# Block 1's small matrix products issued as wholes, one microsecond behind the weight products

## The chip, the cores and the metric

The kernel is one program on one core of a Trainium2 chip. Its engines work side by side: PE multiplies matrices, ACT and DVE work on elements, POOL does a few scalars, SP issues the transfers from memory. The metric is the time of one execution in microseconds (us) on the device, lower is better. The kernel before takes 1691.05 us (median of 3 runs, 1690.16 to 1691.24).

## What is computed

Two layers of a "first block" and two of a "second block" on 256 tokens of width 1024, in float32. The change concerns the first half of the first block, the mixer, which occurs twice (once a layer):

```
h = rmsnorm(x, g_pre_mix);  z = h @ w_in            # 1024 -> 2660 columns
o_moba = softmax attention(rope(qa), rope(ka), va)  # 4 heads of 64, causal
log_f  = log_sigmoid(z_fg + b_forget);  cum = cumsum(log_f, tokens)
o_fox  = softmax attention(qb, kb, vb, + cum[t] - cum[s])
o_mla  = softmax attention from low-rank q and k,v (rmsnorm, w_mla_q_up, w_mla_kv_up)
o_dil  = dilated attention, one masked softmax      # 4 heads of 64
x = x + rmsnorm(concat(o_moba, o_fox, o_mla, o_dil) @ w_out, g_post_mix)
```

Behind it comes a gated feed-forward layer, and the two layers of the second block follow with feed-forward, convolution and pooling. With 256 tokens in tiles of 128, each of the four attentions has two halves of queries, h = 0 (128 keys) and h = 1 (256 keys): eight attentions in a mixer.

## The kernel before, in words

Weights are float32. Each weight unit (128 x 1024) is fetched by SP into a `raw` tile, ACT rounds it to a high part (`wh`), DVE forms the remainder (`wl`), and PE makes three products for one: high by high, high by low, low by high. These are the weight products. Everything else on PE in the mixer is small: transposes against an identity (`idt`, L296), scores q·k (`qk` tiles), weights of the softmax by values (`w` by `vmf`, `vc`, `vd`), and the running sum of the forget gates (`lf` by `cs`).

The order of all instructions is made when the program is built, by a small planner (class `Order`). Every piece of work is a generator that yields one `Op` at a time; the planner keeps a heap, and takes the operation whose start plus `bias` is least, where the start is reckoned from costs written in the code (`mm`, `tr`, `act`, `tt` and so on). Weight products carry a bias of 0.02 (`B_MAIN`); the small products of the mixer carry 0. What comes out is a fixed queue for each engine; on the chip each engine goes through its queue in order, and semaphores hold it where an input is not there yet.

`block1` holds the mixer. Its main generator yields the weight products of each projection (`proj`: latent parts, moba q and k, values of moba and fox, fox q and k, the two low-rank products, dilated q and k, dilated values), then `w_out`, which takes the attentions' outputs in the order moba, fox (h = 0, then 1), low-rank, dilated (h = 0, then 1), 12 weight products each. Chains spawned beside it do the rest: `qkchain`, `foxchain`, `upchain` turn a projection into transposed q and k (`qk`), `cumchain` makes the running sum that fox needs, and `attend` spawns one or two `group`s for each half: scores into a PSUM bank, mask, row maximum, exponentials, reciprocal and scaling into an `lg` tile, transposes into a bank, a copy out of it (`pt`), and then, in `attend`, the products with the values and the split of the result into `mH`, `mL`, which `w_out` reads. There are 8 PSUM banks (`banks`), handed out in the order of asking; the scores of moba and dilated heads use 64 rows of PE each, of alternating halves (`hd % 2`), and the value products 64 columns.

A row of the trace named `lf,cs` is the running sum, `w,vmf` the value products of moba and fox, `w,vc` those of the low-rank attention, `w,vd` of the dilated one. `mH00` is the high part of moba's or fox's output of h = 0.

Of the kernel before, what the change touches and what calls it, by code (L numbers as in the profile page):

```python
# [18 lines left out]
P = 128  # L19
D = 1024  # L20
S = 256
# [11 lines left out]
CST_CAU, CST_DIL, CST_U, CST_IC = 0, 128, 384, 640  # L33
# [10 lines left out]
B_R2 = 0.1  # L44
B_MAIN = 0.02
B_EDGE = -0.1
B_SPLIT = (-0.5, 0.0, 0.2, 0.8)


# [227 lines left out]
def body(ctx, tc, x, positions, wu, wm, wq_up, wkv_up, rows, feat, gfeat, cst, cid, out, nsub=99):  # L277
# [8 lines left out]
    def view(t):  # L286
        return t if isinstance(t, bass.AP) else t[:]

    def mm(o, l, r, start, stop, bias=B_MAIN, fp32=False, half=None):
        o, l, r = view(o), view(l), view(r)  # L290
        c = (4 if fp32 else 1) * r.free_size() / 2400 + 0.0027
        return Op("e", c, (o,), (l, r), lambda: nc.tensor.matmul(o, l, r, start=start, stop=stop), bias, half)  # L292

    def tr(o, i):
        o, i = view(o), view(i)
        return Op("e", 0.1094, (o,), (i,), lambda: nc.tensor.transpose(o, i, idt[:, :P]))  # L296

    def act(o, i, f, bias_=0.0, **kw):
        o, i = view(o), view(i)
        c = (0.052 if i.tensor.name.startswith("bank") else 0.093) + i.free_size() / 1200  # L300
        ins, outs = [i], [o]
        for k in ("scale", "bias"):
            if k in kw and not isinstance(kw[k], float):
                c += 0.093
                ins.append(view(kw[k]))
        if "accum_out" in kw:
            c += 0.093
            outs.append(view(kw["accum_out"]))
        return Op("a", c, outs, ins, lambda: nc.scalar.activation(o, i, f, **kw), bias_, None, f)  # L309
# [72 lines left out]
    cs = one.tile([P, CST_N], F32, name="cs")  # L382
# [12 lines left out]
    def small(n=1):  # L395
        smn[0] += 1
        return smt[smn[0] % len(smt)][:, :n]
# [63 lines left out]
    def split_bias(i):  # L461
        def f():
            ahead = i - st["use"]
            return B_SPLIT[0] if ahead <= 0 else B_SPLIT[1] if ahead < 2 else B_SPLIT[3] if ck.urgent else B_SPLIT[2]
        return f
# [69 lines left out]
    def hidden(n, h, i, src, g):  # L535
# [14 lines left out]
        for j in range(4):  # L550
            kt, o = 4 * i + j, kb[j % 2][:, j * P:(j + 1) * P]
            yield act(hH[:, kt, :], o, AF.Copy, scale=g[:, kt:kt + 1])
            ck.spawn(low(kt, o), bias=B_EDGE)

    def pre_norm(h, n):
# [16 lines left out]

        ts_ = [ck.spawn(part(n, h, i, xx[:, hs[i]], g), bias=B_EDGE) for i in range(2)]
        for t in ts_:
# [10 lines left out]
    def boundary(h, y, half, nxt, eps=None):  # L585
# [8 lines left out]
        a = yield from sumsq(y[0], c / 32)  # L594
        ty = [ck.spawn(gained(0), bias=B_EDGE)]
        a = [a, (yield from sumsq(y[1], c / 32))]
        ms = small()
        yield stt(ms, a[0], c * c * EPS if eps is None else eps, a[1], OP.add, OP.add)
        ty.append(ck.spawn(gained(1), bias=B_EDGE))
        r = small()  # L600
# [3 lines left out]
        if nxt is not None:  # L604
            t = ck.spawn(pre_norm(h, nxt), bias=B_EDGE)
        for i in range(2):
# [53 lines left out]
    def ffn(n_, half, nxt, fp):  # L660
# [117 lines left out]
        for f, c, h in order:  # L778
            yield from f(c, h)
            if f is down and c == NCH - 1:  # L780
                hready[h] = ck.spawn(boundary(h, yacc[h], half, nxt, ep[n_ % 2][h]), bias=B_EDGE)

# [38 lines left out]
    def block1(n_, l, ap, tabs, trope, nxt):  # L821
# [13 lines left out]
        def group(grp, h, q, k, scale, mask, PT, deps, tiled):  # L835
            for t in deps:
                yield t
            nb, hb = h + 1, len(grp)
            wN, w = P * nb, P * nb * hb
            sp = yield banks  # L840
            for i, hd in enumerate(grp):
                yield mm(sp[:, i * wN:(i + 1) * wN], q(hd, h), k(hd, wN), True, True, 0.0, True,
                         hd % 2 if tiled else None)
            lg = yield lgs
            l3 = lg[:, :w].rearrange("p (i n) -> p i n", i=hb)
            s3 = sp[:, :w].rearrange("p (i n) -> p i n", i=hb)
            m = mask[h]
            mN = m.shape[-1]
            mb = m.rearrange("p (o n) -> p o n", o=1).to_broadcast([P, hb, mN])
            if mN < wN:  # L850
                yield act(l3[:, :, :wN - mN], s3[:, :, :wN - mN], AF.Copy)
            yield add(l3[:, :, wN - mN:], s3[:, :, wN - mN:], mb)
            banks.put(sp)
            mx = small(4)
            yield rmax(mx[:, :hb], l3)
            nm = small(4)
            yield ts(nm[:, :hb], mx[:, :hb], -scale, None, OP.mult)
            sm_ = small(4)
            for i in range(hb):
                yield act(l3[:, i, :], l3[:, i, :], AF.Exp, bias=nm[:, i:i + 1], scale=scale,  # L860
                          accum_out=sm_[:, i:i + 1])
            rc = small(4)
            yield recip(rc[:, :hb], sm_[:, :hb])
            for i in range(hb):
                yield ts(l3[:, i, :], l3[:, i, :], rc[:, i:i + 1], None, OP.mult)
            tb = yield banks
            for c in range(hb * nb):
                yield tr(tb[:, c * P:(c + 1) * P], lg[:, c * P:(c + 1) * P])
            lgs.put(lg)
            pt = yield pts  # L870
            yield act(pt[:, :w], tb[:, :w], AF.Copy)
            banks.put(tb)
            for i, hd in enumerate(grp):
                PT[hd] = (pt, i * wN)

        def attend(kt0, h, q, k, v, scale, mask, rowtiled, deps, vdeps, fin):
            if rowtiled:
                groups = [[0, 2], [1, 3]]
            else:
                groups = [[0, 1, 2, 3]] if h == 0 else [[0, 1], [2, 3]]  # L880
            PT = {}
            gs = [ck.spawn(group(g, h, q, k, scale, mask, PT, deps, rowtiled)) for g in groups]
            for t in gs + vdeps:
                yield t
            ob = yield banks
            for s in range(1):
                for hd in range(4):
                    rr = (hd % 2) * 64
                    o = ob[rr:rr + 64, (hd // 2) * P:(hd // 2 + 1) * P]
                    pt, off = PT[hd]  # L890
                    for s in range(h + 1):
                        yield mm(o, v(hd, s), pt[:, off + s * P:off + (s + 1) * P], s == 0, s == h, 0.0, True, hd % 2)
            for pt in {id(p): p for p, _ in PT.values()}.values():
                pts.put(pt)
            fin()
            mH, mL = mix[h][kt0 // 4]
            yield from evac_split(ob[:, :256].rearrange("p (a t) -> p a t", a=2), mH[:, kt0 % 4:kt0 % 4 + 2, :],
                                  mL[:, kt0 % 4:kt0 % 4 + 2, :])
            banks.put(ob)
# [14 lines left out]
        def qkchain(h, b, T):  # L914
            yield tk["tab", h]
            z = yield zs
            yield from rope(z.rearrange("p (n a d) -> p n a d", n=8, a=2),
                            b.rearrange("p (n a d) -> p n a d", n=8, a=2), t64r[h], 8, 32, lambda: banks.put(b))
            tb = yield banks
            for k in range(4):  # L920
                yield tr(tb[:, k * P:(k + 1) * P], z[:, k * P:(k + 1) * P])
            zs.put(z)
            yield act(T[:, :, h * P:(h + 1) * P], tb.rearrange("p (a t) -> p a t", a=4), AF.Copy)
            banks.put(tb)
# [24 lines left out]
        lf = ap.tile([P, 8], F32, name="lf")  # L949
# [58 lines left out]
        def cumchain():  # L1008
            for h in range(2):
                yield ck.flag("fg", n_, h)  # L1010
            yield stt(lf, fg, -1.0, fg, OP.mult, OP.min)
            yield act(lf, lf, AF.Exp)
            yield act(lf, lf, AF.Ln, bias=1.0)
            yield stt(lf, fg, 0.0, lf, OP.min, OP.subtract)
            ct = yield banks
            yield mm(ct[:, 0:4], cs[:, CST_U:CST_U + P], lf[:, 0:4], True, True, 0.0, True)
            yield mm(ct[:, 4:8], cs[:, CST_U + P:CST_U + S], lf[:, 0:4], True, False, 0.0, True)
            yield mm(ct[:, 4:8], cs[:, CST_U:CST_U + P], lf[:, 4:8], False, True, 0.0, True)
            yield act(cum, ct[:, :8].rearrange("p (h n) -> p h n", h=2), AF.Copy, scale=-8.0)
            banks.put(ct)  # L1020
        tcum = ck.spawn(cumchain())
# [12 lines left out]
        def headchain(h, z, T, n):  # L1034

            tb = yield banks
            for k in range(4):
                yield tr(tb[:n, k * P:(k + 1) * P], z[:, k * n:(k + 1) * n])
            zs.put(z)
            yield act(T[:n, :, h * P:(h + 1) * P], tb[:n].rearrange("p (a t) -> p a t", a=4), AF.Copy)  # L1040
            banks.put(tb)
# [25 lines left out]
        for h in range(2):  # L1067
            tk["af", h] = ck.spawn(attend(2, h, lambda hd, hh, T=Tq: T[:65, hd, hh * P:(hh + 1) * P],
                                          lambda hd, n, T=Tk: T[:65, hd, :n], vget("f"), 0.125, cau, False,
# [535 lines left out]
```

## Time and profile before

| | |
|---|---|
| median of 3 runs | 1691.05 us |
| the profiled execution | 1689.79 us, of which span of the trace 1688.0 us |
| PE busy | 1676.5 us (99%) |
| DVE, ACT busy | 1258.6 us (75%), 1027.2 us (61%) |
| granted clock of PE | 0.998 of full speed |
| chain that ended last | PE 96% |
| first mixer of the trace | until some 122 us; the second from some 303 to 411 us |

A busy PE in the trace is one that has a matmul in flight; a matmul's record is longer than its share of the pipeline, so what a product costs is read from one start to the next.

### The profile page before, as it was taken

To read this page: it belongs to the slowest core of one execution; us is meant where nothing else is said; L and a number is where in the kernel's file an instruction comes from. 1 tells how busy PE (TensorE), PEld (TensorE's weight loads), DVE (VectorE), ACT (ScalarE), POOL (GpSimd) and SP (SyncE) were. 2 spreads that over 40 slices of the span, in tenths; PEclk is the share of its full clock that TensorE was granted. 3 is DMA by queue.
4 is the path that set the end of the run, shared out by engine and by line. 5 is a ranking of instruction groups with operands and counts; after the bars stand their busy time and mean duration, and the time that the engine had idled before them with its cause. 6 is when DMAs were issued, how large, how long until landed. Compare 5 with 4: busy or idle time off the path is not lost.

```text
span 1688.0 us, 25148 instructions
## 1 busy us (share of the span) xinstructions
PE 1676.5 (99%) x9417; PEld 1494.6 (89%) x9417; DVE 1258.6 (75%) x1927; ACT 1027.2 (61%) x1749; POOL 35.8 (2%) x72
## 2 busy tenths in 40 slices
PE   8999999999999999999999999999999999999998
PEld 7788998878999899988998899989998899889997
DVE  6878765877877587657898787668765789878663
ACT  7867554786755475546656575557554666567552
POOL 1000000100000000000000000000000000000000
PEclk9999999999999999999999999999999999999999
DMA  8357764524875477655656586647664665648650
GB/s 279 103 169 245 248 203 150 165 90 138 278 235 198 137 239 235 200 162 197 205 186 200 168 290 228 197 141 248 215 209 140 224 201 181 204 165 302 217 168 25
DMA packets 92283, 328.46 MB, mean 195 GB/s; under 512 B 11008, under 2 KB 12032, under 8 KB 91904
## 3 DMA queue, kind: packets, MB, share of 16 engines
q1 hardware_dynamic: 92160, 326.86, 58.5%
q8 instruction: 73, 1.20, 0.3%
q14 instruction: 50, 0.41, 0.1%
HBM read 325.77 MB, written 1.05 MB: 194 GB/s over the span
## 4 chain that ended last, share of the span: by engine, by line
PE 96%; ACT 1%; DMA 1%; DVE 1%; issue 1%; SPq 0%; DVEq 0%; POOLq 0%; POOL 0%; ACTq 0%
PE bank L292 93%; PE bank L296 3%; DMA raw<-in_wu_dram 1%; ACT wh L309 1%; DMA raw<-in_wm_dram 0%; DVE wl L314 0%; ACT hX L309 0%; ACT L309 0%; SPq L367 0%; ACT junk L309 0%; DVE sm L342 0%; ACT qk L309 0%; DVE x L337 0%; DVE w L314 0%; DVEq L1601 0%
## 5 line engine op out<-in xcount | busy, mean ns | idle before, releaser
L314 DVE TENSOR_TENSOR wl<-raw,wh 128x1024 fp32r<-128x1024 f32 (+1 forms) x472 | 565.2, 1207 | 142.9 <-ACT wh L309 139.3
L292 PE MATMUL bank<-hX,wh 128*128 128x512 f32 x1736 | 572.7, 382 | 0.0
L309 ACT ACTIVATE wh<-raw 128x1024 fp32r<-128x1024 f32 (+1 forms) x472 | 487.3, 1042 | 110.0 <-DMA raw<-in_wu_dram 59.8
L292 PE MATMUL bank<-hX,wl 128*128 128x256 f32 x1736 | 473.7, 273 | 0.0
L292 PEld LDWEIGHTS bank<-hX,wh 128*128 128x128 f32 x1736 | 328.1, 189 | 45.5
L292 PEld LDWEIGHTS bank<-hX,wl 128*128 128x128 f32 x1736 | 333.2, 192 | 1.0
L292 PE MATMUL bank<-wh,hX 128*128 128x512 f32 (+2 forms) x960 | 287.2, 375 | 0.0
L309 ACT ACTIVATE scr<-bank 128x256 f32<-128x256 f32 x288 | 109.2, 379 | 245.4 <-PE bank L292 245.3
L292 PE MATMUL bank<-hX,xh 128*128 128x512 f32 x696 | 230.3, 382 | 0.0
L292 PEld LDWEIGHTS bank<-wh,hX 128*128 128x128 f32 x960 | 177.8, 190 | 21.9 <-issue 1.5
L314 DVE TENSOR_TENSOR xl<-raw,xh 128x1024 fp32r<-128x1024 f32 x139 | 168.7, 1222 | 33.0 <-ACT xh L309 32.0
L314 DVE TENSOR_TENSOR scr<-scr,bank 128x256 f32<-128x256 f32 x288 | 120.4, 418 | 97.2 <-ACT scr L309 97.1
L292 PE MATMUL bank<-hX,xl 128*128 128x256 f32 x696 | 189.7, 273 | 0.0
L292 PE MATMUL bank<-wl,hX 128*128 128x512 f32 (+2 forms) x480 | 179.5, 374 | 0.3 <-DVE wl L314 0.3
L309 ACT ACTIVATE xh<-raw 128x1024 fp32r<-128x1024 f32 x139 | 144.9, 1053 | 16.5 <-DMA raw<-in_wu_dram 13.2
L292 PEld LDWEIGHTS bank<-hX,xh 128*128 128x128 f32 x696 | 131.5, 189 | 18.4
L292 PEld LDWEIGHTS bank<-hX,xl 128*128 128x128 f32 x696 | 133.6, 192 | 0.4
L292 PE MATMUL bank<-wh,fH 128*128 128x512 f32 x320 | 121.6, 380 | 0.0
L292 PE MATMUL bank<-wl,fH 128*128 128x512 f32 x320 | 121.4, 380 | 0.0
L292 PE MATMUL bank<-wh,fL 128*128 128x512 f32 x320 | 121.3, 379 | 0.0
L292 PEld LDWEIGHTS bank<-wl,hX 128*128 128x128 f32 x480 | 91.2, 190 | 11.2 <-DVE wl L314 0.8
L292 PE MATMUL bank<-xh,fH 128*128 128x512 f32 x208 | 79.1, 380 | 0.0
(148 smaller groups left out, 1929.0 us busy)
## 6 DMA issues: line engine op xcount, KB each, us to landing
raw<-in_wu_dram SPq DMA_DIRECT2D x596, 512.0 KB, 4.8
gpost<-in_rows_dram SPq DMA_DIRECT2D x10, 512.0 KB, 7.2
raw<-in_wm_dram SPq DMA_DIRECT2D x7, 356.0 KB, 3.8
bg<-in_rows_dram SPq DMA_DIRECT2D x2, 1024.0 KB, 4.7
x<-in_x_dram SPq DMA_DIRECT2D x4, 256.0 KB, 5.6
out_dram<-x SPq DMA_DIRECT2D x4, 256.0 KB, 2.0
raw<-in_wkv_up_dram SPq DMA_DIRECT2D x2, 256.0 KB, 3.7
raw<-in_wq_up_dram SPq DMA_DIRECT2D x2, 192.0 KB, 4.4
```

The lines of the kernel that those rows point to most:

```text
L292: return Op("e", c, (o,), (l, r), lambda: nc.tensor.matmul(o, l, r, start=start, stop=stop), bias, half)
L296: return Op("e", 0.1094, (o,), (i,), lambda: nc.tensor.transpose(o, i, idt[:, :P]))
L309: return Op("a", c, outs, ins, lambda: nc.scalar.activation(o, i, f, **kw), bias_, None, f)
L314: lambda: nc.vector.tensor_tensor(o, a, b, op=op), bias)
```

## The change

`whole(ops, bias)` makes one `Op` of several matmuls: the planner gives it one start, the sum of the costs (half the cost for matmuls of half an array), and emits all of them in a row. In `block1` the scores of a group, the transposes of a tile and the value products of an attention are yielded as one whole with a bias of 1.0 (`B_LATE`), the three products of the running sum as one with 2.0. The three transposes of the latent parts (`mlachain`) stay single. No other operation is added or removed; the operands are the same.

```
+B_LATE = 1.0
...
+    def whole(ops, bias=0.0):
+
+        return Op("e", sum(o.cost * (1 if o.half is None else 0.5) for o in ops), [a for o in ops for a in o.outs],
+                  [a for o in ops for a in o.ins], lambda: [o.fn() for o in ops], bias)
...
-            for i, hd in enumerate(grp):
-                yield mm(sp[:, i * wN:(i + 1) * wN], q(hd, h), k(hd, wN), True, True, 0.0, True,
-                         hd % 2 if tiled else None)
+            yield whole([mm(sp[:, i * wN:(i + 1) * wN], q(hd, h), k(hd, wN), True, True, 0.0, True,
+                            hd % 2 if tiled else None) for i, hd in enumerate(grp)], B_LATE)
...
-            for c in range(hb * nb):
-                yield tr(tb[:, c * P:(c + 1) * P], lg[:, c * P:(c + 1) * P])
+            yield whole([tr(tb[:, c * P:(c + 1) * P], lg[:, c * P:(c + 1) * P]) for c in range(hb * nb)], B_LATE)
...
-                    for s in range(h + 1):
-                        yield mm(o, v(hd, s), pt[:, off + s * P:off + (s + 1) * P], s == 0, s == h, 0.0, True, hd % 2)
...
+                for s in range(h + 1):
+                    pv.append(mm(o, v(hd, s), pt[:, off + s * P:off + (s + 1) * P], s == 0, s == h, 0.0, True, hd % 2))
+            yield whole(pv, B_LATE)
...
-            for k in range(4):
-                yield tr(tb[:, k * P:(k + 1) * P], z[:, k * P:(k + 1) * P])
+            yield whole([tr(tb[:, k * P:(k + 1) * P], z[:, k * P:(k + 1) * P]) for k in range(4)], B_LATE)
...
-            yield mm(ct[:, 0:4], cs[:, CST_U:CST_U + P], lf[:, 0:4], True, True, 0.0, True)
-            yield mm(ct[:, 4:8], cs[:, CST_U + P:CST_U + S], lf[:, 0:4], True, False, 0.0, True)
-            yield mm(ct[:, 4:8], cs[:, CST_U:CST_U + P], lf[:, 4:8], False, True, 0.0, True)
+            yield whole([mm(ct[:, 0:4], cs[:, CST_U:CST_U + P], lf[:, 0:4], True, True, 0.0, True),
+                         mm(ct[:, 4:8], cs[:, CST_U + P:CST_U + S], lf[:, 0:4], True, False, 0.0, True),
+                         mm(ct[:, 4:8], cs[:, CST_U:CST_U + P], lf[:, 4:8], False, True, 0.0, True)], 2 * B_LATE)
```

How the queues move, at three places of the first mixer. First PE at the running sum (`lf` by `cs`), before:

```order
L292 MATMUL bank6_134<-wh1_69,hX_66 128x512 x2
L292 MATMUL bank6_134<-wl1_70,hX_66 128x512
L292 MATMUL bank7_135<-lf_259,cs_99 128x4 x3
L292 MATMUL bank6_134<-wh1_69,hX_66 128x512
L292 MATMUL bank6_134<-wh2_71,hX_66 128x512
```

and now, between the first twelve products of `w_out` and the next:

```order
L293 MATMUL bank1_129<-wh7_81,mL00_236 128x512
L297 MATMUL bank5_133<-idt_100,w4_247 128x128 x4
L293 MATMUL bank7_135<-lf_259,cs_99 128x4 x3
L297 MATMUL bank0_128<-idt_100,w1_244 128x128 x4
L297 MATMUL bank7_135<-idt_100,w0_243 128x128 x4
L297 MATMUL bank6_134<-idt_100,w3_246 128x128 x2
```

The running sum stood among the products of the values' projection and now stands behind all projections, with 205 weight products more ahead of it. Second, PE around the first product of `w_out` (it reads `mH00`), before:

```order
L292 MATMUL bank7_135<-wh5_77,hX_66 128x256
L292 MATMUL bank0_128<-qk5_255 128x128
L292 MATMUL bank4_132<-qk5_255 128x128
L292 MATMUL bank0_128<-qk5_255 128x128
L292 MATMUL bank4_132<-qk5_255 128x128
L292 MATMUL bank2_130<-qk5_255 128x256
L292 MATMUL bank1_129<-qk5_255 128x256
L292 MATMUL bank2_130<-qk5_255 128x256
L292 MATMUL bank1_129<-qk5_255 128x256
L292 MATMUL bank5_133<-wh6_79,mH00_235 128x512
```

and now, at the 13th product of `w_out`, the first that reads fox's output (also `mH00`):

```order
L293 MATMUL bank7_135<-w3_246,vd0_917 64x128
L293 MATMUL bank7_135<-w3_246,vd1_957 64x128
L297 MATMUL bank3_131<-idt_100,w0_243 128x128 x4
L293 MATMUL bank2_130<-w4_247,vmf0_560 64x128 x4
L293 MATMUL bank4_132<-wh8_83,mH00_235 128x512
L293 MATMUL bank4_132<-wl8_84,mH00_235 128x512
```

Before, the first `w_out` product follows the scores of the dilated attention, with the other six attentions done; now the dilated value products and fox's come between the 12th and the 13th. In all 36 small products stand ahead of the first `w_out` product and 83 between the 12th and the 13th, with no weight product among them; 16 more stand between the 36th and the 37th. The second mixer has the same pattern with 30, 89 and 12. Third, ACT, whose queue holds `cum` (the copy of the running sum), before:

```order
L309 ACTIVATE lf_259<-lf_259 128x8
L309 ACTIVATE wh5_77<-raw4_89 128x1024
L309 ACTIVATE cum_516<-bank7_135 128x8
L309 ACTIVATE wh6_79<-raw0_85 128x1024
L309 ACTIVATE wh7_81<-raw1_86 128x384
```

and now:

```order
L315 ACTIVATE w6_249,sm48_184<-w6_249,sm46_182 128x128 x2
L315 ACTIVATE w4_247<-bank0_128 128x512
L315 ACTIVATE cum_516<-bank7_135 128x8
L315 ACTIVATE w1_244<-bank6_134 128x512
L315 ACTIVATE w6_249<-bank5_133 128x512
L315 ACTIVATE w0_243,sm56_192<-w0_243,sm54_190 128x256 x2
L315 ACTIVATE qk2_252<-bank5_133 65x4x128
```

The copy stood among roundings of weights and now stands among exponentials (`w,sm`) and copies of the attentions.

## Rows read from the trace of the kernel before

**Rows 1.** The page's line of PE: busy us, share of the span, instructions.

```profile
PE 1676.5 (99%) x9417; PEld 1494.6 (89%) x9417; DVE 1258.6 (75%) x1927; ACT 1027.2 (61%) x1749; POOL 35.8 (2%) x72
```

**Rows 2.** Who PE waited for, whole run: us in total, times, longest.

```profile
PE bank L296 <- DMA x<-in_x_dram: 2.3, 1, 2.3
PE bank L292 <- DVE lf L337: 1.0, 1, 1.0
PE bank L296 <- DVE w L331: 0.8, 1, 0.8
```

**Rows 3.** Windows, 44.5 to 112: PE in all, transposes (L296) alone, scores (qk) alone.

```profile
44.50:112.00 67.50, 67.50 (x453) 1.00 0.40 130
44.50:112.00 67.50, 16.30 (x102) 1.00 0.40 130
44.50:112.00 67.50, 9.60 (x64) 1.00 0.40 130
```

**Rows 4.** Timeline of PE, 53.6 to 87: start us, us, instructions; single and grouped small products.

```profile
54.07 0.59 PE L292 MATMUL bank<-wh,hX 128*128 128x512 f32 x2
...
54.51 0.38 PE L292 MATMUL bank<-wl,hX 128*128 128x512 f32 x1
...
55.73 0.68 PE L292 MATMUL bank<-wh,hX 128*128 128x512 f32 x2
...
81.49 0.66 PE L292 MATMUL bank<-w,vc 128*64 128x128 f32 x8
82.08 0.48 PE L292 MATMUL bank<-wl,hX 128*128 128x512 f32 x1
82.40 0.59 PE L292 MATMUL bank<-wh,hX 128*128 128x512 f32 x2
...
83.91 0.60 PE L296 MATMUL bank<-idt,w 128*128 128x128 f32 x4
84.27 0.46 PE L292 MATMUL bank<-wh,hX 128*128 128x512 f32 x1
...
85.75 1.15 PE L292 MATMUL bank<-w,vc 128*64 128x128 f32 x16
86.82 0.48 PE L292 MATMUL bank<-wl,hX 128*128 128x512 f32 x1
```

**Rows 5.** Timeline, 97 to 112.5: the dilated attention, on PE, and its last DVE operation.

```profile
97.57 1.58 PE L292 MATMUL bank<-qk 64*128 64x128 f32 x16
...
99.08 0.48 PE L292 MATMUL bank<-wh,mH 128*128 128x512 f32 x1
...
110.87 1.09 PE L292 MATMUL bank<-w,vd 128*64 128x128 f32 x12
...
111.88 0.48 PE L292 MATMUL bank<-wh,mL 128*128 128x512 f32 x1
...
112.41 0.42 DVE L314 TENSOR_TENSOR mL<-bank,mH 128x256 fp32r<-128x256 f32 x1 [0.28 <-ACT mH L309]
```

**Rows 6.** ACT by form, 30 to 125: busy us, mean ns; idle before, releaser.

```profile
L309 ACT ACTIVATE wh<-raw 128x1024 fp32r<-128x1024 f32 x24 | 25.2, 1053 | 5.9 <-DMA raw<-in_wu_dram 3.0 <-PE bank L292 1.5 <-DVE wl L314 1.3
L309 ACT ACTIVATE w<-w,sm 128x256 f32<-128x256 f32 x16 | 7.9, 500 | 0.0
L309 ACT ACTIVATE w<-w,sm 128x128 f32<-128x128 f32 x16 | 6.2, 395 | 3.5 <-DVE sm L331 3.4
...
L309 ACT ACTIVATE w<-bank 128x512 f32<-128x512 f32 x10 | 5.8, 592 | 1.2 <-PE bank L296 1.0
L309 ACT ACTIVATE w<-bank 128x256 f32<-128x256 f32 x14 | 5.0, 378 | 0.6 <-PE bank L296 0.3
```

**Rows 7.** DVE by form, 40 to 125, same columns.

```profile
L314 DVE TENSOR_TENSOR wl<-raw,wh 128x1024 fp32r<-128x1024 f32 x19 | 22.8, 1220 | 3.8 <-ACT wh L309 3.7
L342 DVE TENSOR_REDUCE sm<-w 128x2 f32<-128x512 f32 x8 | 5.2, 676 | 0.0
```

**Rows 8.** Window at the start: busy us of PE to POOL, granted clock, DMA share, GB/s.

```profile
10.00:11.00 1.00, 1.00 (x7) 0.94 (x5) 0.87 (x2) 1.00 (x5) 0.00 (x0) 0.50 1.04 416
```

More of the change, by code (lines that the diff above doesn't have):

```diff
@@ L885, in attend @@
             ob = yield banks
[L886 to L890, printed above, removed]
-                    for s in range(h + 1):
-                        yield mm(o, v(hd, s), pt[:, off + s * P:off + (s + 1) * P], s == 0, s == h, 0.0, True, hd % 2)
+            pv = []
+            for hd in range(4):
+                rr = (hd % 2) * 64
+                o = ob[rr:rr + 64, (hd // 2) * P:(hd // 2 + 1) * P]
+                pt, off = PT[hd]
+                for s in range(h + 1):
+                    pv.append(mm(o, v(hd, s), pt[:, off + s * P:off + (s + 1) * P], s == 0, s == h, 0.0, True, hd % 2))
+            yield whole(pv, B_LATE)
             for pt in {id(p): p for p, _ in PT.values()}.values():
@@ L1036, in headchain @@
             tb = yield banks
-            for k in range(4):
-                yield tr(tb[:n, k * P:(k + 1) * P], z[:, k * n:(k + 1) * n])
+            yield whole([tr(tb[:n, k * P:(k + 1) * P], z[:, k * n:(k + 1) * n]) for k in range(4)], B_LATE)
             zs.put(z)
```

## The prediction

> **What bounds the kernel now.** I read the page's busy line first [rows 1]: PE is busy for 1676.5 of 1688.0 us, DVE for 75% and ACT for 61% of it. The waits of PE come next [rows 2]: the three largest it has in its queue after the warm-up are 2.3 us at the very start (the tokens), 1.0 us for the input of the running sum in the first mixer and 0.8 us for a transpose in the second. So nothing but PE's own queue sets the time, and whatever the change does shows in two places: how long the same products take on PE when they stand in another order, and how long PE now stands idle. Feed-forward layers and the second block, whose queues do not move, keep PE full, so an idle microsecond in a mixer is not given back later.
>
> **What the change can remove.** A weight product of 512 columns takes 0.22 us from start to start (two from 54.07 to 54.51) [rows 4]. In the window 44.5 to 112 of the first mixer PE has 453 records and no gap [rows 3]: 102 transposes, 64 of scores, 96 of value products (48 products by the code, two records each; the row of 16 is the eight of an h = 1 half), and so 191 of weight products: 131 of 512 columns, 48 of 256 (dilated values) and 12 of 384 (low-rank). At 0.216, 0.109 and 0.163 us, by columns, these are 28.3 + 5.2 + 2.0 = 35.5 us, and the small products have the other 32.0 us.
>
> What would they take if each kind stood in unbroken rows? Transposes gain nothing: four single ones with four weight products between fill 54.51 to 55.73, 1.22 us, less 4 x 0.22 leaves 0.09 each, and four in a row take 0.36 us (83.91 to 84.27), also 0.09 each [rows 4]. Inside longer rows I reckon 0.11, half a 512-column slot (an estimate). Value products do gain: 8 records take 0.59 us and 16 take 1.07 [rows 4], and the weight product behind is late by 0.1 (82.08 to 82.40 instead of 0.22), so 0.69 and 1.17: some 0.2 us of each stop is stepping in and out. All transposes at 0.11 are 11.2 us; value products 4 x (0.69 + 1.17) = 7.4; the 32 half-array score records, two rows of 16 at 1.51 + 0.1 (97.57 to 99.08) [rows 5], 3.2; the 32 whole-array ones at 0.11 (128 columns) and 0.22 (256), 5.3. Sum 27.1, so at most 4.9 us of the 32.0 is the price of scattering. At least 1.4 us goes: half-array rows come in some 16 stops before and 9 now, and 7 x 0.2 is that. I take 3.5 us, and 0.9 us for the wait of rows 2 that each mixer had. Removed: 4.4 us a mixer, between 2.3 and 5.8.
>
> One rule of the Trainium skill speaks against the new order of the half-array scores. The row of 12 value records [rows 5] has two products on one half of the columns, then two on the other, then two on the first, and takes 1.01 us, not the 1.3 of twelve at 0.11, so halves overlap even when two of one half come first. The page "TensorE: Matmul & The Clock Gate", section "Part 3: Packing small matmuls", says that a load of weights overlaps a running matmul only where the row groups differ; by it a whole, whose two score products sit on the same 64 rows, would lose the overlap, and 4 products of 128 and 4 of 256 columns would take 2.6 us for 1.6, twice a mixer. The sum by that rule is 4 us higher over both mixers; the sum here keeps the row's overlap.
>
> **What the change adds.** A handicap of 1.0 us puts a small product behind every weight product that is ready, so they go only when the weight products cannot. The order shows where: at the three places where the projections ask for a bank and none is free, and in `w_out`, where the weights wait for the attentions. Before, at the first `w_out` product six attentions were done and the dilated one was covered: its scores begin at 97.57 and its last remainder ends at 112.83 [rows 5], 15.3 us for one attention, while 40 of `w_out`'s weight products run. Now most softmax work of all eight attentions stands between the end of the projections and the 13th `w_out` product, with only 12 weight products for cover. I put T = 0 at the end of the last projection.
>
> PE's work from T = 0 to the 13th product: 52 transposes 5.7, running sum 0.7, whole-array scores 1.8 + 3.5, half-array scores 1.6, value products 4 x 0.69 + 3 x 1.17 = 6.3, 12 weight products 2.6: 22.2 us. ACT's queue in the same stretch, all of it behind the last projection and ahead of the `mH` that the 13th product reads: 15 copies of 256 columns at 0.38, 11 of 512 at 0.59, 12 exponentials of 128 at 0.395, 12 of 256 at 0.50, two roundings at 1.05, the sum's copy 0.2 [rows 6]: 5.7 + 6.5 + 4.7 + 6.0 + 2.1 + 0.2 = 25.2 us. With the remainder on DVE (0.42) [rows 5] and hand-overs, 26 us even if ACT never waits, so PE idles at least 26 - 22.2 = 3.8 us.
>
> But it does wait, since PE, ACT and DVE hand one chain to each other. Going through the three queues by the rows' durations: two roundings and two remainders (1.05 and 1.22 each) [rows 6, 7] stand ahead of the first masks, moba's h = 0 output is ready at T = 9.9; 12 products end at 12.0; the running sum ends at 13.3 and its copy, behind the exponentials, at 14.5; fox's transposes end at 18.0, their copies behind more exponentials at 19.3 and 21.5; scores 22.2 to 23.0; mask and maximum (0.68 each) to 25.5; four exponentials to 27.3; scaling to 28.4; the transposes wait on PE behind the dilated value products, whose last copy ACT ends at 29.0, and end at 30.4; copy 31.3, values 32.0; on ACT four exponentials of the next half stand ahead of `mH`, 34.0; remainder 34.9. That is 12.7 us idle. I take 11, near the chain, since a single attention alone took 15.3 us in the trace.
>
> The other stops: at the 37th product the transposes (half of them 0.45), two copies (1.2), eight value products (1.17), `mH` and `mL` (0.8) and 0.8 of hand-overs make 4.4 us, of which PE works 2.1: 2.3 idle. At the banks PE resumes when ACT, behind a rounding, has copied up to three tiles, 1.05 + 0.59 + 0.38 + 0.59 = 2.6 us and 0.4 of hand-overs, against 1.8 us of transposes: 1.2 idle, twice; and where the low-rank product wants a bank that DVE frees behind five remainders (5 x 1.22) [rows 7], some 1.4. Sum 6.1, from 2 to 7; I take 5.
>
> **The sum.** A mixer gains 16 of idle and loses 4.4: +11.6, both +23 us. The profiled execution took 1689.8, 1.3 under the median; on the median, 1691 + 23 = 1714, called 1713. A difference under 0.2% (3.4 us) cannot be told from none here.
>
> **Rivals.**
> - ACT sets the stop, not the chain: idle 3.8 + 3 = 7, less 4.4, +2.6 a mixer: 1696 (1692 to 1701). For it: much of the softmax work may be done under the projections, where ACT has slack (61% over the run) [rows 1]. Against: ACT's 25.2 us lie behind the last projection by the order. 14%.
> - Faster: the rows of small products find their inputs ready and PE never idles; then 4.9 + 0.9 us go in each mixer: 1679. It needs idle under 5.8 us a mixer, and the running sum's successors (transposes, scores, softmax, transposes, values) to fit under other work of PE. Against it the 15.3 us of one attention. 7%.
> - The clock falls in the stops. After the 2.3 us wait at the start [rows 2] the granted clock was half (0.50, the 1.2 GHz level) [rows 8]. The chain above has two idle stretches of some 2 us near T = 28 and 33. If it falls, part of 12 us of small products and the 12 weight products double, of which I reckon 5.5 us on the path, +11: 1724. 10%.
> - The planner's order has no effect on time, gain and idle cancel: 1691. 3%.
>
> **Numbers.** Forecast 66%, its own range 1703 to 1724. Faster by over 0.2%: 7%. Within: 3% and the foot of the first rival, 5%. Slower: 88%. The range 1698 to 1726 leaves out the faster case, no change and part of the first rival.
>
> **What would show it.** PE's waits in the changed profile should name ACT and DVE with some 30 us in total, most in two stretches of some 35 us between the last projection and the 13th `w_out` product; ACT near 75% busy there; the weight products ahead of it at 0.216 with hardly a small product between. It is wrong if PE stays at 99%, if the idle lies elsewhere, or if small products cost PE as much as before.

## The result and the profile after

The changed kernel takes 1714.92 us (median of 5 runs, 1713.71 to 1716.15) against 1691.05 us (1688.78 to 1691.24) of the kernel before on the same chip: ratio 1.0148, 95% interval 1.0137 to 1.0158, or some 24 us slower. The profiled execution took 1713.71 us, with a span of 1711.9 us, 23.9 more than that of before.

First the busy line and the chain of the page after, which answer to [rows 1]:

```profile
PE 1682.4 (98%) x9417; PEld 1501.8 (88%) x9417; DVE 1260.6 (74%) x1927; ACT 1026.4 (60%) x1749; POOL 35.7 (2%) x72
...
PE 94%; ACT 2%; DVE 2%; issue 1%; DMA 1%; SPq 0%; DVEq 0%; POOLq 0%; POOL 0%; ACTq 0%
```

The same 9417 products, and PE is busy only 5.9 us longer, yet the span grew by 23.9: most of the loss is time in which PE has nothing in flight. The waits of PE over the whole run, where before only a start and two of a microsecond stood [rows 2] (us in total, times, longest):

```profile
PE bank L293 <- ACT qk L315: 4.2, 4, 2.3
PE bank L293 <- ACT w L315: 4.1, 7, 0.8
PE bank L293 <- ACT mH L315: 3.6, 4, 2.1
PE bank L297 <- DMA x<-in_x_dram: 2.2, 2, 1.6
PE bank L297 <- DVE w L337: 1.7, 3, 0.9
PE bank L297 <- ACT cum L315: 1.4, 1, 1.4
...
PE bank L297 <- ACT w L315: 0.9, 2, 0.7
```

PE now waits for what ACT and DVE hand it in an attention: transposed q and k (`qk`), the softmax and its copies (`w`), the outputs (`mH`), the copy of the running sum (`cum`). Windows show where. The columns are window, its length, busy us of PE, weight load, DVE, ACT and POOL, granted clock, DMA share, GB/s:

```profile
55.00:62.00 7.00, 4.66 (x30) 4.05 (x28) 3.78 (x9) 6.06 (x12) 0.00 (x0) 1.00 0.96 349
81.00:89.40 8.40, 7.65 (x60) 6.16 (x59) 7.51 (x18) 5.45 (x15) 0.00 (x0) 1.00 0.57 186
92.00:114.00 22.00, 16.56 (x132) 13.26 (x131) 14.59 (x49) 16.08 (x56) 0.00 (x0) 0.84 0.00 1
119.30:123.10 3.80, 2.55 (x28) 1.90 (x26) 2.48 (x3) 2.72 (x5) 0.00 (x0) 1.00 0.27 79
...
394.00:415.20 21.20, 17.54 (x140) 13.48 (x139) 15.55 (x55) 15.34 (x56) 0.00 (x0) 0.92 0.01 1
420.60:424.00 3.40, 2.31 (x24) 1.56 (x23) 2.62 (x3) 2.19 (x4) 0.00 (x0) 1.00 0.16 52
```

They are the stops: at a bank (55 to 62), before the first product of `w_out` (81 to 89.4), before the 13th (92 to 114, 394 to 415) and before the 37th (119 to 123, 421 to 424). In the long ones no engine is full: PE 75%, ACT 73%, DVE 66% of 92 to 114. Three engines that are all partly idle are the mark of a chain that goes through them in turn. PE's timeline of that stop (start, us, operation; in brackets the idle time ahead of it and its releaser):

```profile
81.10 0.38 PE L297 MATMUL bank<-idt,w 128*128 128x128 f32 x2
...
84.69 0.72 PE L293 MATMUL bank<-qk 64*128 64x128 f32 x8
85.34 1.43 PE L297 MATMUL bank<-idt,w 128*128 128x128 f32 x8
86.70 1.25 PE L293 MATMUL bank<-qk 64*128 64x256 f32 x8
87.88 0.66 PE L293 MATMUL bank<-w,vmf 128*64 128x128 f32 x8
89.16 0.46 PE L293 MATMUL bank<-wh,mH 128*128 128x512 f32 x1 [0.63 <-DVE w L320]
...
92.43 0.73 PE L293 MATMUL bank<-lf,cs 128*128 128x4 f32 x6
94.56 1.11 PE L297 MATMUL bank<-idt,w 128*128 128x128 f32 x8 [1.40 <-ACT cum L315]
...
102.96 2.79 PE L293 MATMUL bank<-qk,qk 65*128 65x128 f32 x16
...
109.71 0.66 PE L297 MATMUL bank<-idt,w 128*128 128x128 f32 x4
111.11 0.66 PE L293 MATMUL bank<-w,vmf 128*64 128x128 f32 x8 [0.75 <-ACT w L315]
113.88 0.48 PE L293 MATMUL bank<-wh,mH 128*128 128x512 f32 x1 [2.11 <-ACT mH L315]
```

The running sum (`lf,cs`) starts at 92.43, and all of fox follows it: transposes, scores at 102.96, last transposes at 109.71, values at 111.11, and the 13th product at 113.88. Its last link on ACT:

```profile
110.46 0.60 ACT L315 ACTIVATE w<-bank 128x512 f32<-128x512 f32 x1 [0.26 <-PE bank L297]
...
111.49 0.51 ACT L315 ACTIVATE w<-w,sm 128x256 f32<-128x256 f32 x1 [0.43 <-DVE sm L337]
...
112.97 0.49 ACT L315 ACTIVATE w<-w,sm 128x256 f32<-128x256 f32 x1
113.37 0.19 ACT L315 ACTIVATION_READ_ACCUMULATOR w<-w,sm 128x1 f32 x1
113.47 0.36 ACT L315 ACTIVATE mH<-bank 128x256 fp32r<-128x256 f32 x1
```

The values are done at 111.77, but the rounding to `mH` stands behind four exponentials (111.49 to 113.47) of a half that nobody waits for yet.

**Where the 24 us went.** I added up PE's starts from one record to the next, from the 101st weight product (30.58 us before, 30.51 after) to the transposes behind the first mixer (121.94, 133.60), and between the transposes around the second (297.22 to 410.38; 308.87 to 434.36). The first grew by 11.7 us, the second by 12.3. A stop costs its idle time, and also the drain: the last record ahead of it counts as busy for some 0.2 us after the next start was due. Where the granted clock was 0.50, half of the time counts as clock.

| both mixers, us | before | after | difference |
|---|---|---|---|
| idle | 1.8 | 18.8 (30 times) | +17.0 |
| drain ahead of it | 0.3 | 5.5 | +5.2 |
| lost to half clock | 0 | 6.1 | +6.1 |
| small products | 56.9 | 58.5 | +1.6 |
| weight products above 0.216, 0.163, 0.15, 0.109 us by size | 10.8 | 4.8 | -6.0 |

The sum is +23.9.

### The profile page after: what moved, and what is told of

It is laid out like the page before. It is cut to its first block, busy times and chain, and to the rows that moved or that the text cites. A ratio compares the mean times of both kernels' runs of the same rounds, so it can differ in the third digit from the quotient of the medians.

```text
span 1711.9 us, 25165 instructions
## 1 busy us (share of the span) xinstructions
PE 1682.4 (98%) x9417; PEld 1501.8 (88%) x9417; DVE 1260.6 (74%) x1927; ACT 1026.4 (60%) x1749; POOL 35.7 (2%) x72
## 3 DMA queue, kind: packets, MB, share of 16 engines
HBM read 325.77 MB, written 1.05 MB: 191 GB/s over the span
## 4 chain that ended last, share of the span: by engine, by line
PE 94%; ACT 2%; DVE 2%; issue 1%; DMA 1%; SPq 0%; DVEq 0%; POOLq 0%; POOL 0%; ACTq 0%
PE bank L293 92%; PE bank L297 2%; ACT w L315 1%; ACT wh L315 1%; DVE wl L320 0%; DVE sm L348 0%; DVE w L320 0%; DMA raw<-in_wu_dram 0%; DMA raw<-in_wm_dram 0%; DVE w L337 0%; ACT qk L315 0%; DVE mL L320 0%; DVE scr L320 0%; SPq L373 0%; ACT mH L315 0%
## 5 line engine op out<-in xcount | busy, mean ns | idle before, releaser
L320 DVE TENSOR_TENSOR xl<-raw,xh 128x1024 fp32r<-128x1024 f32 x139 | 168.6, 1222 | 34.9 <-ACT xh L315 34.1
```

The source lines that it names most:

```text
L320: lambda: nc.vector.tensor_tensor(o, a, b, op=op), bias)
```

## The experiments

Ratios are to the kernel before on the same chip. A ratio of 0.001 is 1.7 us.

**1. Grouping alone.**

```
-B_LATE = 1.0
+B_LATE = 0.0
```

> Grouping kept, both handicaps set to 0 (of the four kinds of group each product still goes out in a row). Theory (the loss comes from the handicap, which pushes all softmax chains behind the last projection): the running sum goes early again, PE has no stop, small products stand in some 36 rows; 1684 to 1690 us, PE waits under 4 us in all. Rival 1 (grouping itself costs, by lost overlap of half-array scores and longer rows): at least 1699, a third of the 24 us or more. Rival 2 (the loss is mostly TensorE's clock at half level): about 1691 too, with no spell at half level except at start and end.

Measured: 1684.33 us, ratio 0.9970 (0.9959 to 0.9982), 4.9 us faster than before. Its waits of PE in the mixers and a window over the whole first one:

```profile
PE bank L293 <- DVE lf L343: 1.8, 1, 1.8
```

```profile
42.00:120.00 78.00, 78.00 (x517) 65.57 (x515) 64.93 (x166) 58.54 (x146) 0.55 (x1) 1.00 0.46 149
```

One wait, and from 42 to 120 no idle time and a full clock. Without a handicap the grouping is a gain, so rival 1 falls: on top of the groups the handicap costs 30 us (from 0.9970 to 1.0148).

**2. The handicap alone.** The products carry 1.0 (the running sum's 2.0) one by one:

```
-        return Op("e", sum(...), ..., lambda: [o.fn() for o in ops], bias)
+        for o in ops:
+            o.bias = bias
+            yield o
...
-            yield whole(pv, B_LATE)
+            yield from whole(pv, B_LATE)
```

> The handicap of 1.0 (2.0 for the running sum) on single products, nothing grouped. Theory (handicap): the same starved order, 1712 to 1722 us. Rival 1 (grouping costs): at most 1700 us, since nothing is grouped. Rival 2 (clock): as the handicap if PE stands idle in the same places, with 10 us or more of half level.

Measured: 1707.92 us, 1.0114 (1.0100 to 1.0128). The handicap alone costs 19 us, with no groups; 4 us less than I had expected. The clock was at half level in the mixers only from 89.21 to 92.62, at most 1.7 us of the 19, so the clock is not the cause of the loss either. Runs 1 and 2 together show one thing more: under the handicap the grouping turns from a gain of 5 us into a cost of 6 (1.0114 to 1.0148). The mixers of the changed kernel have 13.65 us at half level where run 2 has 3.41, which is most of it, and some 2 us more of idle time.

**3. The running sum early.**

```
-  ... lf[:, 4:8], False, True, 0.0, True)], 2 * B_LATE)
+  ... lf[:, 4:8], False, True, 0.0, True)], 0.0)
```

> Everything as in the changed kernel, but the running sum's group has a handicap of 0 instead of 2.0. Theory (the chain running sum, fox transposes, scores, softmax, transposes, values sets the end of the stop): the sum goes out among the projections, the fox chain starts some 20 us sooner, and the stop before the 13th product of w_out shrinks; 1698 to 1708 us. Rival (ACT's queue of 25 us behind the last projection alone sets the stop): no change beyond 2 us, 1712 to 1717.

Measured: 1702.43 us, 1.0078 (1.0063 to 1.0093), in the theory's range. The sum starts at 33.99 instead of 92.43, and 12 us come back, nearly all of them in the first mixer: its last product of `w_out` starts at 126.66 instead of 136.92, that of the second mixer at 426.44 instead of 437.68, which is 1 us more. In the second mixer a row of 54 small products still stands ahead of `w_out`, PE is idle for 3.8 us in it, and the clock is at half level for 6.83 us. The run does not tell the chain from ACT's queue, since the early sum also takes fox's share of ACT's work out of the stretch from the last projection to the 13th product:

```profile
88.20:97.96 9.76, 9.76 (x83) 8.15 (x82) 8.15 (x25) 9.47 (x25) 0.00 (x0) 1.00 0.43 150
```

ACT has 9.47 us of work there, against 24.0 in the changed kernel (window under "Added in the long stop").

**4. A smaller handicap.** `B_LATE` 0.2, so 0.4 for the running sum.

> The changed kernel with handicaps of 0.2 (0.4 for the running sum) instead of 1.0 (2.0). Theory (a handicap in a greedy planner is a rank, since a weight product of 0.2 us is always ready: a switch and not a dose): 1708 to 1718 us. Rival (a dose): a fifth of the loss, about 1696 us.

Measured: 1691.41 us, 1.0012 (1.0003 to 1.0021). My expectation fell, and the rival's 1696 was not met either. The order of the first mixer looked like the changed kernel's (rows of 45 and 84 small products before the 1st and the 13th product of `w_out`; in the second mixer the rows are 32, 32 and 36), but the stop is shorter:

```profile
83.10 1.13 PE L293 MATMUL bank<-qk 64*128 64x256 f32 x4
84.16 0.83 PE L293 MATMUL bank<-lf,cs 128*128 128x4 f32 x6
...
91.47 0.72 PE L293 MATMUL bank<-qk,qk 65*128 65x128 f32 x5
```

The running sum goes at 84.16, ahead of the twelve products and not behind them, so its copy and fox's transposes are done under other work, and fox's first scores start at 91.47 instead of 102.96. The 84 products take 17.2 us (90.82 to 108.01), 2.5 of them idle, where the changed kernel's 83 take 22.1 (91.78 to 113.88). A long row of small products costs less when its inputs are there sooner; against run 1 the handicap of 0.2 still costs 7 us.

**5. and 9. The running sum late, the rest less.** Handicap 2.0 for the running sum's group; for all others 0.2 (5) or 0 (9):

```
-  ... lf[:, 4:8], False, True, 0.0, True)], 2 * B_LATE)
+  ... lf[:, 4:8], False, True, 0.0, True)], 2.0)
```

> Handicap 0.2 for the groups as in the run that took 1691.4 us, but 2.0 for the running sum's group as in the changed kernel. Theory A (the late running sum is half of the loss, as the run with only the sum early took 12 us less than the changed kernel): 1700 to 1706 us. Theory B (what costs is the 1.0 on the groups: the planner takes the least start plus handicap, so a weight product that can start within 1.0 us goes ahead of a small one that could start now, and PE, in order, stands still): 1689 to 1694 us.

> Groups with a handicap of 0 (as in the run that took 1684.3 us), and 2.0 for the running sum's group alone. Theory (the late running sum leaves one chain, fox, to run behind the projections with little cover): 7 to 16 us over that run, 1692 to 1700 us, with PE waiting on DVE and ACT between the 12th and the 13th product of w_out. Rival (all eight attentions must be late for a stop): within 3 us of it, 1684 to 1687.

Measured: 1706.98 us, 1.0101 (1.0084 to 1.0118), 1 us over the range of theory A and far from B's, and 1699.72 us, 1.0059 (1.0045 to 1.0072), in the theory's range. The stop of the latter, with everything but fox on time:

```profile
98.44 0.83 PE L293 MATMUL bank<-lf,cs 128*128 128x4 f32 x6
99.74 1.09 PE L297 MATMUL bank<-idt,w 128*65 128x128 f32 x8 [0.47 <-DVE w L356]
101.08 2.89 PE L293 MATMUL bank<-qk,qk 65*128 65x128 f32 x16 [0.25 <-ACT qk L315]
106.51 2.23 PE L297 MATMUL bank<-idt,w 128*128 128x128 f32 x8 [2.54 <-DVE w L337]
108.66 1.12 PE L293 MATMUL bank<-w,vmf 128*64 128x128 f32 x8
...
110.43 0.46 PE L293 MATMUL bank<-wh,mH 128*128 128x512 f32 x1
```

From the sum to the 13th product 12.0 us, the bare length of one attention's chain (with the clock at half level from 106.97), and PE waits 2.54 us for its softmax alone. Run 5 has the same 12.0 us there (102.10 to 114.09). The runs stand in a table of two handicaps:

| ratio to before | groups 0 | groups 0.2 | groups 1.0 |
|---|---|---|---|
| sum 0 | 0.9970 | | 1.0078 |
| sum 0.4 | | 1.0012 | |
| sum 2.0 | 1.0059 | 1.0101 | 1.0148 |

Down a column the late sum costs 15, 15 and 12 us; along a row the groups' 1.0 costs 18 us with the sum early, 15 with it late. Such a difference of two ratios is uncertain by some 3 us, so over the whole run these are two causes of about one size that nearly add. Mixer by mixer they do not: with the groups at 0 the late sum costs 7 us in each mixer (up to the last product of `w_out`), with the groups at 1.0 it costs 10 in the first and 1 in the second. That the second cause depends on the size of the handicap can be read in the planner: it takes the least start plus handicap, so a weight product that can start within the handicap goes ahead of a small one that could start now, and PE keeps that order even where it has to stand still. No run isolates this.

**6. ACT or the chain.** In `group`, the copy out of the transposes' bank goes to DVE:

```
-            yield act(pt[:, :w], tb[:, :w], AF.Copy)
+            yield copy(pt[:, :w], tb[:, :w])
```

> The changed kernel with the copies out of the transposes' banks (26 a mixer, 12 us of ACT in the stop) on DVE instead of ACT. Theory (a chain PE, ACT, DVE that waits at each hand-over, with DVE's own queue in the stop as long as ACT's): within 6 us of the changed kernel, 1708 to 1718 us. Rival (ACT's queue alone sets the stop): 5 us or more less in each mixer, 1704 us or less.

Measured: 1711.99 us, 1.0130 (1.0115 to 1.0145). The window of the stop:

```profile
82.00:115.50 33.50, 27.67 (x207) 21.81 (x205) 30.59 (x93) 19.25 (x70) 0.00 (x0) 0.95 0.15 48
```

ACT has 19.25 us of 33.50 now, against 24.0 of 32.8 in the changed kernel (its window stands further down), and the stop is no shorter. But DVE has become nearly full (30.59), and the order moved: the running sum now goes at 90.01, ahead of the first product of `w_out` at 92.30. So the run alone can't tell. What speaks against ACT as the floor is the changed kernel itself: in its stop ACT is idle for 8.8 of the 32.8 us.

**7. and 8. Shorter links.** The reciprocal and the scaling in `group` left out, so the rows of the softmax are not normalised, in the changed kernel and in the kernel before:

```
-            rc = small(4)
-            yield recip(rc[:, :hb], sm_[:, :hb])
-            for i in range(hb):
-                yield ts(l3[:, i, :], l3[:, i, :], rc[:, i:i + 1], None, OP.mult)
```

> The changed kernel without the reciprocal and the scaling of the softmax rows (left out, so the attentions' outputs are not normalised); some 3 us of DVE per attention half less. Theory (chain): each link that PE waits for gets about 1 us shorter, 1703 to 1711 us. Rival (ACT alone sets the stop): 1712 to 1717 us.

> The kernel before without the reciprocal and the scaling of the softmax rows (left out in the same way). All theories: these operations lie beside PE's full queue, so nothing is gained: 1687 to 1692 us.

Measured: 1709.73 us, 1.0117 (1.0102 to 1.0133), and 1685.11 us, 0.9973 (0.9962 to 0.9983). The first is in the chain theory's range, but the control, too, took 5 us less than its own base, where I had expected nothing. PE had only 1.8 us of idle time to win in its mixers; by the account above its small products took 52.6 us in both mixers instead of 56.9, in another order. So the pair says nothing for the chain: leaving out work off the path still moves a planner's order.

**10., 11. and 12. What of the grouping gains.** All without handicap: 10 yields the transposes one by one again, 11 all but the value products, 12 keeps all groups at -0.1.

```
+    def each(ops, bias=0.0):
+        for o in ops:
+            o.bias = bias
+            yield o
...
-            yield whole([tr(tb[:, c * P:(c + 1) * P], lg[:, c * P:(c + 1) * P]) for c in range(hb * nb)], B_LATE)
+            yield from each([tr(tb[:, c * P:(c + 1) * P], lg[:, c * P:(c + 1) * P]) for c in range(hb * nb)], B_LATE)
```

> No handicap; scores, values and the running sum grouped, the transposes single as before. Theory (transposes gain nothing from standing in a row): as the run with all grouped, 1683 to 1687 us. Rival (the rows of transposes carry the gain): 1687 to 1691, as before.

> No handicap; only the value products of an attention grouped, all else single as before. Theory (what is gained is the stepping in and out of half-array products): most of the 5 us, 1684 to 1688 us. Rival (the gain is the place of the running sum and chance of order): 1688 to 1691.

> All groups kept, with a handicap of -0.1 (-0.2 for the running sum), so that a small product goes ahead of a weight product that could start up to 0.1 us sooner. Theory: fewer stops than with 0, PE waits up to 0.1 us for some of them; 1682 to 1687 us, at best 2 us under the run with 0. Rival (PE stands idle for groups that are not ready): 1686 to 1692.

Measured: 1684.21 us, 0.9967 (0.9955 to 0.9980); 1682.64 us, 0.9961 (0.9949 to 0.9974); 1684.46 us, 0.9975 (0.9965 to 0.9984). The second is 1.4 us under its expected range. The intervals overlap: no run shows transposes gaining from standing in a row, and with the value products alone grouped the whole gain is there. Run 8 moved as much by another order alone, so the trace has to say where this gain lies: from start to start the value products take 16.8 us of both mixers before, and 12.9 to 13.2 in runs 1, 10, 11 and 12. In run 8, with nothing grouped, they take 14.2. So some 4 us of the gain are at the value products, but how much of it another order without groups would have had stays open. The page of 11 has PE at

```profile
PE 1668.4 (99%) x9417; PEld 1491.2 (89%) x9417; DVE 1258.8 (75%) x1927; ACT 1026.6 (61%) x1749; POOL 35.9 (2%) x72
```

8.1 us under [rows 1]; the span, 1682.5 us, is 5.5 shorter. This version, one kind of group and no handicap, beats both kernels: 1682.64 us against 1689.77 of before beside it.

## Why the prediction was right, step by step

**The bound.** PE's queue; what moved the time was PE's idle time and the order in its queue. In run 1 the same products in another order, with no more idle time than before, took 4.9 us less.

**Removed: 4.4 us a mixer said, 3.1 found.** Weight products lost 6.0 us of steps in and out, small ones gained 1.6, and the waits that before had (1.8 idle) are gone: 6.2 us for both. The mis-sized term is the 3.5 us of scattering, 2.2 by the table, inside its bounds of 1.4 to 4.9. With the grouping alone it was 2.3 (small products 53.5 instead of 56.9 us, weight products 9.6 instead of 10.8), and the 4.9 us of run 1 are nearly all of that. That transposes gain nothing and values do fits runs 10 and 11. One sign of being wrong that the prediction named, small products that cost PE as much as before, is there if they are taken by themselves (58.5 us against 56.9); the gain lies in the weight products behind them, whose late start the prediction had counted with the stops of small ones.

**The rule weighed against the trace.** In the first mixer the two score groups of each size stand behind one another, on both halves: 8 records of 256 columns go from 86.70 to 87.88, and with the 0.65 us of the 128s (84.69 to 85.34) the four products of each size take 1.8 us, near the 1.6 of the row. In the second mixer the groups of 256 columns stand apart:

```profile
389.65 1.13 PE L293 MATMUL bank<-qk 64*128 64x256 f32 x4
...
393.97 1.13 PE L293 MATMUL bank<-qk 64*128 64x256 f32 x4
395.02 0.45 PE L293 MATMUL bank<-w,vmf 128*64 128x128 f32 x4
```

Four records on one half take 1.05 us (393.97 to 395.02), nearly as long as eight on both (1.18). So a group alone on one half does lose the overlap, about 1 us for the two of this mixer, and the row's overlap holds only where the other half's products stand next to it. That 1 us is part of the 1.6 by which the small products became longer. But it is not the load of weights that fails to overlap: the four start at 393.97, 394.29, 394.50 and 394.72, so the last two steps are 0.22 us, and whole-array records of 256 columns start 0.22 apart as well (104.07 to 105.37). What is missing is the other half running beside them: the eight of the first mixer start at 86.71, 86.82, 87.03, 87.14 and so on, twice as often. The Trainium skill's page "TensorE: Matmul & The Clock Gate", "Part 3: Packing small matmuls", says that a load of weights overlaps a running matmul only where the row groups differ; the steps of 0.22 us on one half do not agree with that, though the price that the prediction worked out from it was met where a group stood alone.

**Added in the long stop: the chain.** From the end of the last projection, T = 0 at 81.1, by the waypoints of the prediction and the trace of the first mixer:

| | said | found |
|---|---|---|
| twelve products of `w_out` done | 12.0 | 10.9 |
| copy of the sum done, next transposes start | 14.5 | 13.5 |
| fox's scores | 22.2 to 23.0 | 21.9 to 24.6 |
| fox's last transposes done | 30.4 | 29.3 |
| values done | 32.0 | 30.7 |
| 13th product | 34.9 | 32.8 |

The second mixer took 30.3 (384.84 to 415.13). The order of the links is that of the sum, down to the four exponentials ahead of `mH`. Of the two idle stretches of some 2 us near T = 28 and 33 the second is there (2.11 us), while the first has 0.27 (at 108.69). The windows of the whole stretch in both mixers have DVE with as much work as ACT; I had summed only ACT's and PE's queues:

```profile
81.10:113.90 32.80, 26.61 (x201) 21.20 (x199) 24.38 (x78) 24.02 (x80) 0.00 (x0) 0.90 0.15 49
384.84:415.13 30.29, 26.23 (x196) 20.40 (x194) 22.89 (x73) 22.90 (x79) 0.00 (x0) 0.94 0.11 36
```

ACT's 73% and 76% are the near 75% that was to be seen there.

**The size of the idle time: 32 us said, 24.3 found** (18.8 idle, 5.5 drain). Most of the miss lies in the long stops: 11 us each were said, and the windows above leave 6.2 and 4.1 idle, beside their share of the drain and of the clock. Elsewhere 8.5 us are idle where 10 were said: the stops at the 37th product have 1.25 and 1.09 where 2.3 was said, and those at the banks 2.9 and 2.7 a mixer where 3.8 was said, with one of 2.34 in place of 1.2.

**The clock, put down as a rival at 10%, came in beside the forecast**, at half the price: 6.1 us (11 said), and not only in the stop. Idle time said 8 too much, the clock 6 too little, the gain 3 too much: the time was right to 2 us (1713 said, 1714.92 measured) because these nearly cancel. The way and the place of the loss were foreseen; that the number is so close is luck.

**The other rivals.** ACT as the floor (1696): in the long stop of the changed kernel ACT has no work for 8.8 of 32.8 us, which speaks against it; runs 3 and 6 do not tell. Faster (1679): its condition, rows of small products with ready inputs, is what the grouping has without the handicap, and there 1682 to 1684 us were measured.

## What to carry to other kernels

Where one engine is the bound and others feed it through chains, do the small products of a long chain as early as they are ready: a rank behind ready bulk work is paid back at the first point where the bulk work needs the chain's end. Group what shares a step in and out (here half-array products), and see that the two halves stand side by side; do it without changing the rank. The rows of small products alone do not tell a stop: in the first mixer runs 4 and 5 have much the same rows (45 and 84, 42 and 79), but from the 101st weight product to the last of `w_out` they take 96.3 and 106.2 us. The only edit between them is the handicap of one three-product sum.

## What had not been expected of the hardware

The granted clock of PE fell in the stops of the changed kernel. Windows over three stretches at half level (same columns as above):

```profile
95.50:102.34 6.84, 5.92 (x38) 4.63 (x36) 4.48 (x13) 5.40 (x16) 0.00 (x0) 0.50 0.00 0
361.75:365.16 3.41, 3.41 (x10) 2.68 (x9) 2.06 (x12) 3.37 (x11) 0.00 (x0) 0.50 0.70 241
402.71:406.12 3.41, 3.41 (x25) 2.75 (x24) 0.83 (x4) 3.02 (x9) 0.00 (x0) 0.50 0.00 0
```

The middle one fell on weight products of a projection, behind two waits of under a microsecond:

```profile
360.00 0.64 PE L297 MATMUL bank<-idt,w 128*96 128x128 f32 x4 [0.85 <-ACT qk L315]
361.21 0.48 PE L293 MATMUL bank<-wh,hX 128*128 128x512 f32 x1 [0.58 <-ACT qk L315]
...
361.75 1.05 PE L293 MATMUL bank<-wh,hX 128*128 128x512 f32 x2
362.60 0.63 PE L293 MATMUL bank<-wl,hX 128*128 128x512 f32 x1
363.02 1.06 PE L293 MATMUL bank<-wh,hX 128*128 128x512 f32 x2
```

Two products from 361.75 to 362.60 are 0.43 us each for 0.22, the 1.2 GHz level while PE was busy throughout. The wait of 2.34 us at 59 in the same run was followed by no half level, while the 2.3 us at the start of before, which ended at 8.42, were followed by one [rows 8]. So the longest single wait does not tell where the clock falls, and what it costs is paid by the products behind the stop.
